# Last half of the output projection: first weight sums by VectorE, six more raw buffers, and a look-ahead of fourteen pieces

## The chip, the cores and the metric

The kernel runs on one core of a Trainium2 chip. Its time is the device time of one execution in microseconds (us), and a run is described by the median of several executions. PE is the matrix engine (TensorE; PEld are its weight loads), DVE is VectorE, ACT is ScalarE, POOL is GpSimd. SP is the engine that issues most of the loads.

## What is computed

One block of a diffusion transformer for 512 latent tokens, 256 context tokens and a width of 2048, all in fp32. What matters here is its end:

```python
y_a = (attn * silu(z_a)) @ w_pa
y_b = (fourier_mix(u_b) * silu(z_b)) @ w_pb
y = (sigmoid(g_a) * y_a + sigmoid(g_b) * y_b) @ w_o
out = rmsnorm(x + gate * y, final_g)
```

The input to `w_o` is called the merged matrix below: 512 tokens by 2048. The output projection is the product of the merged matrix with `w_o` (2048 by 2048). The gates `g_a`, `g_b` come from a product of the same kind, of the normed input with 4096 columns of `w_in`.

## The kernel before

**Every product three times.** An fp32 operand is split into a high part (ScalarE rounds it, line 131) and a low part (VectorE subtracts, line 132). A product is the sum of three matmuls, high by high, high by low and low by high (lines 251 to 253). So each piece of weights, 128 x 1024 or 512 KB, is loaded into a *raw* buffer, split into a pair of tiles (`whi`, `wlo`) and multiplied from there. For a piece of the output projection that is 12 matmuls of 512 columns.

**Seven products for eight.** The gates (four groups, 0 to 3) and the output projection (groups 4 and 5, each half of the columns of `w_o`) are multiplied by a scheme of the Strassen kind: 1024 x 512 blocks of weights are combined, the tokens' matrix is combined into *forms* (A11, Z5, A12, S2, S3, S4, A22), and seven products called P1, Q5, P2, Q6, P7, Q3, Q4 take the place of eight. Each product has four pieces. `class Group` (line 790) runs them; its order in group 5 is `ONE_GROUP`, that of group 4 `OUT_GROUP`. The products of the last group:

- P1 with A11, Q5 with Z5, Q6 with S2 and Q4 with A22 use the weights of a *chain*: four buffers R0 to R3, one for each piece. P1 loads one block into R (line 165, by SP). Q5 needs R plus a second block, Q6 that plus a third, Q4 that plus a fourth.
- P2 (A12) and Q3 (S4) use one block as it is.
- P7 (S3) uses the sum of two blocks: two raw buffers are loaded and VectorE adds them (line 198), then the sum is split.

**Two ways of adding to the chain.** In the general case the next block is added by an accumulating DMA, issued on POOL as soon as R has been split (line 207). For the stages listed in `by_dve`, the block is loaded by SP into a raw buffer like any other, and VectorE adds it to R (line 198) before the split. In the kernel before, the gates do that for stage 1, which is Q5 (`BY_DVE_GATES`), and the output projection for none (`BY_DVE_OUT`).

**The list of pieces.** All pieces, and the blocks of `x` that are added at the end, stand in one list, `todo`, in the order in which they are used. `load_more` moves pieces from its head to `ahead`, up to eight, as long as there are raw buffers for them. `start_load` picks the raw buffers from `raw_pools` by counting which are still held by pieces in `ahead`; a piece whose weights are in R holds none. `get(key)` hands out the next piece: it splits the first few pieces of `ahead` (as many as there are pairs of split tiles, four in the output projection) and starts new loads. A tile's memory is handed on when its last use is over, and each engine's order of issue is made when the kernel is built, from dependencies and the order of the program.

**Raw buffers.** Four in `wp` and two in `rp` exist during the whole second half; two more (`evp`) during the gates, and three more tiles of `hm` (`extra`) during the first three of the four chunks of branch A, which lies between the gates and the output projection. In groups 4 and 5 there are six.

**Tiles for everything else.** `take` and `give` hand out tiles of 4 KB per partition from the list `free`: the oldest free one first. The last group takes tiles from it for its results and for rows of the gate and of the final norm. `free_form` (line 1252) gives back the four tiles of a form when its product in the last group is over.

**The end.** After P2, P7 and Q3, `out_done` multiplies a result by the gate (line 1200), adds `x` (line 1202) and lets `finish_chunk` square it (line 1174) and scale it (line 1180). `prepare` (lines 1185 and 1186) does its part for the results of Q3 and Q4 ahead of time. Lines 821 hold the sums that turn the seven products into results. `last` (lines 1238 to 1249) finishes the last 512 columns for 256 tokens, 128 at a time, and stores them.

```python
part = lambda i: w[CHAIN[i][0], CHAIN[i][1], pc]
stream(key, [part(what)] if what in by_dve else [], 1024, 2, stage=what, pc=pc,
       nxt=part(what + 1) if what < 3 and what + 1 not in by_dve else None)
```

Of the kernel before, what the change touches and what calls it, by code (L numbers as in the profile page):

```python
# [50 lines left out]
ONE_GROUP = ("P1", "Q5", "P2", "Q6", "P7", "Q3", "Q4")  # L51
OUT_GROUP = ("P1", "P2", "Q5", "Q6", "P7", "Q3", "Q4")

BY_DVE_GATES, BY_DVE_OUT = (1,), ()

CHUNKS = (0, 2, 1, 3)
BRANCH_A, BRANCH_B = (0, 1, 2, 3, 4, 5), (6, 7)
# [26 lines left out]
def block_kernel(ctx, tc, xT, ctxT, x, c_row, w_ss, w_gate, vecs, qkg, rope, dft_c, dft_s,  # L84
# [9 lines left out]
    hm = sb("hm", KK)  # L94
# [15 lines left out]
    def uid(s):  # L110
        cnt[0] += 1
        return f"{s}{cnt[0]}"
# [22 lines left out]
    todo, ahead = [], []  # L135
    chain, left = [], [0] * 4
    raw_pools, hl_pools = [(wp, RAW, "raw", RAW)], [wp] * HL
# [11 lines left out]
    def stream(key, src, *a, **k):  # L149
        todo.append(Piece(key, src if isinstance(src, list) else [src], *a, **k))  # L150

    def start_load():

        e = todo[0]
        used = [p for a in ahead for p, _ in a.raws]
        free = [p for p in raw_pools for _ in range(p[1] - used.count(p))]
        if len(e.parts) > len(free) or e.stage == 0 and (not chain or left[e.pc]):
            return False
        todo.pop(0)
        for p, src in zip(free, e.parts):  # L160
            raw = p[0].tile([P, 1024], F32, tag=p[2], bufs=p[3], name=uid("wr"))[:, : e.cols]
            nc.sync.dma_start(raw, src)
            e.raws.append((p, raw))
        if e.stage == 0:
            nc.sync.dma_start(chain[e.pc], e.first)
            left[e.pc] = 1
        ahead.append(e)
        return True

    def load_more():  # L170
        while todo and len(ahead) < 8 and start_load():
            pass

    class Halves:
# [38 lines left out]
    def get(key):  # L213
        load_more()
        turn = [e for e in ahead if not e.aside]
        assert turn[0].key == key, (turn[0].key, key)
        for e in turn[: len(hl_pools)]:
            split_piece(e)
        load_more()
        e = turn[0]  # L220
        ahead.remove(e)
        free.extend(p[0::2] for p, _ in e.raws if p in retired)
        return e.raws[0][1] if e.kind == "raw" else e.out
# [10 lines left out]
    free, retired, home = [], [], {}  # L234
# [4 lines left out]
    def take(shape, dt=F32, pool=None):  # L239
        p = next((p for p in free if p[0] is pool), free[0])  # L240
        free.remove(p)
        t = slot_tile(p, shape, dt)
        home[id(t)] = p, t
        return t

    def give(*ts):
        free.extend(home.pop(id(t))[0] for t in ts)

    def mm3(o, ah, al, bh, bl, start, stop, cont=False):

        nc.tensor.matmul(o, ah, bh, start=start, stop=False, skip_group_check=cont)  # L251
        nc.tensor.matmul(o, ah, bl, start=False, stop=False, skip_group_check=cont)  # L252
        nc.tensor.matmul(o, al, bh, start=False, stop=stop, skip_group_check=cont)  # L253
# [54 lines left out]
    def stream_product(name, g, w, by_dve):  # L308

        what = next(p[2] for p in PRODUCTS if p[0] == name)  # L310
        for pc in range(4):
            key = (name, g, pc)
            if isinstance(what, tuple):
                stream(key, [w[a, b, pc] for a, b in what], 1024, 2)
            else:
# [3 lines that stand above are left out]
                todo[-1].first = part(0)  # L319
# [25 lines left out]
            half, c = DONE[name]  # L345
            stream(("x", half, 2 + c), flat(x[half, 2 + c]), 1024, 1, "raw")
    for name in ONE_GROUP:
        stream_product(name, 5, w_o[0], BY_DVE_OUT)
        half, c = {"P2": (0, 0), "P7": (1, 1), "Q3": (1, 0)}.get(name, (0, 0))
        if name == "Q3":  # L350
            stream(("x", 0, 1), flat(x[0, 1]), 1024, 1, "raw")
            todo.insert(len(todo) - 5, todo.pop())
        if name in ("P2", "P7", "Q3"):
            stream(("x", half, c), flat(x[half, c]), 1024, 1, "raw")
# [260 lines left out]
    for t in range(4):  # L615
        s = slice(t * P, (t + 1) * P)
# [56 lines left out]
    for which, half in ((0, 0), (0, 1), (1, 1)):  # L673
# [3 lines left out]
        for pc in range(8):  # L677
# [3 lines left out]
            for k in range(2):  # L681
                kk = 2 * pc + k
                for a, t in zip(accs, toks):
                    s = slice(t * P, (t + 1) * P) if t < 4 else slice((t - 4) * P, (t - 3) * P)
# [7 lines left out]
        for a, t in zip(accs, toks):  # L692
            a = a.rearrange("p (h d) -> p h d", h=4)
            s = slice(t * P, (t + 1) * P)
# [72 lines left out]
    def pair(tag):  # L767
        return ps2.tile([P, 2, 512], F32, tag=tag, bufs=2, name=uid(tag))
# [8 lines left out]
    def job():  # L777
        if jobs:
            jobs.pop(0)()
# [207 lines left out]
    for i in range(NSTEP + 2):  # L987
# [9 lines left out]
        if i % 3 > 0 and i < 3 * KK:  # L997
            q = i // 3 * 2 + i % 3 - 1
# [3 lines left out]
        if i % 3 < 2 and i < 3 * KK:  # L1002
            q = i // 3 * 2 + i % 3
# [65 lines left out]
    def load_gate(which, half, j):  # L1069
        t = take((2, 512), pool=gp)  # L1070
        nc.gpsimd.dma_start(t, g_d[which, half, j].rearrange("p (t c) -> p t c", t=2))
        return t
# [4 lines left out]
    def turn_merged(j, i, tag):  # L1077

        tp = pair(tag)
        for b in range(2):  # L1080
            for t in range(4):
                c = slice((2 * i + b) * P, (2 * i + b + 1) * P)
                nc.tensor.transpose(tp[:, b, t * P : (t + 1) * P], merged[j, t // 2][:, t % 2, c], ident)
        if i == 0:
            raws[j] = [take((4, 256)) for _ in range(2)]
        else:
            give(merged[j, 0], merged[j, 1])
        for h in range(2):
            nc.scalar.copy(raws[j][h][:, 2 * i : 2 * i + 2, :], tp[:, :, 256 * h : 256 * h + 256])
# [24 lines left out]
    def form_job(name, h):  # L1114
        return lambda: form(name, h)

    extra = [(hm, 1, f"s{i}", 1) for i in range(3)]
    for p in extra:
        free.remove(p[0::2])
    raw_pools += extra  # L1120
    for n, j in enumerate(CHUNKS):
        if n == 3:
            retired += extra
            for p in extra:
                raw_pools.remove(p)
                if not any(q == p for e in ahead for q, _ in e.raws):
                    free.append(p[0::2])
        gb = [load_gate(1, h, j) for h in range(2)]
        ga = [load_gate(0, h, j) for h in range(2)]
        accs = [pair("yx"[n % 2]) for _ in range(2)]  # L1130
        for pc in BRANCH_A:
            if n == 0:
                S[pc] = get(("src", pc))
            wh, wl = get(("pab", j, pc))
            sh, sl = S[pc]
            for t in range(4):
                s = slice(t * P, (t + 1) * P)
                for k in range(2):
                    mm3(accs[t // 2][:, t % 2, :], sh[:, k, s], sl[:, k, s], wh[:, k, :], wl[:, k, :],
                        pc == 0 and k == 0, pc == BRANCH_A[-1] and k == 1)  # L1140
            if pc:
                job()
        for h in range(2):
            nc.vector.tensor_tensor(ga[h], accs[h], ga[h], op=ALU.mult)
            nc.vector.tensor_tensor(gb[h], ga[h], gb[h], op=ALU.add)
            merged[j, h] = gb[h]
        give(*ga)
        turned = [lambda j=j, i=i, n=n: turn_merged(j, i, "yx"[n % 2]) for i in range(2)]
        if n == 3:

            waiting = jobs[:]
            jobs[:] = [lambda: load_rows(1), lambda: None] + turned + [form_job("A12", 1)] + waiting
            jobs.extend(form_job(f, 1) for f in ("Z5", "S2", "S4", "A22"))
        else:
            jobs[:] = turned + jobs
            jobs.extend(form_job(f, j % 2) for f in (("A11", "S3"), ("A12", "Z5", "S2", "S4", "A22"))[j // 2])
# [5 lines left out]
    def load_rows(g):  # L1162
        for l, src in ((gates, gs.rearrange("(o k) p -> o (k p)", o=1)), (fgs, final_g)):
            l[g] = take((2, 512))
            nc.scalar.dma_start(l[g], src[:, 1024 * g : 1024 * g + 1024].broadcast_to([P, 1024]))
# [16 lines left out]
    def prepare(t, half, j):  # L1182

        o[half, j] = t
        nc.vector.tensor_tensor(t, t, row(gates, j), op=ALU.mult)  # L1185
        nc.vector.tensor_tensor(t, get_x(half, j), t, op=ALU.subtract)  # L1186
# [65 lines left out]
    def free_form(name):  # L1252
        for h in range(2):
            give(*held.pop((name, h)))
# [9 lines left out]
    for name in ONE_GROUP:  # L1264
        if name == "Q3":

            nc.scalar.activation(mhalf[:, 8:9], ssq[:, 0, 2:3], ACT.Sqrt)
            prepare(last_group.X, 0, 1)
        elif name == "Q4":
            prepare(last_group.Y, 1, 0)  # L1270
        last_group.run(name)
        free_form(next(f for n, f, _, _ in PRODUCTS if n == name))
        if name == "P1":
            load_rows(0)
    while jobs:
        job()

# [80 lines left out]
```

## Time and profile before

| | us |
|---|---|
| median of 3 runs | 1388.69 |
| lowest, highest | 1388.03, 1389.51 |
| the profiled execution | 1388.98 |
| its span | 1387.2 |
| PE busy | 1351.4 |
| DVE busy | 910.7 |
| ACT busy | 630.1 |

The span is what the profiler recorded from the first to the last instruction of that one execution; the 1.8 us beside it lie before and after. In rows of the timeline the columns are the start, the duration, engine, line, operation, the tile written and the tiles read (buffer numbers left out), and in brackets the idle time of the engine just before and what ended it. Rows of waits give total, count and longest. In the rows of a DMA queue the columns are packets, MB, and the time that the packets took as a share of 16 engines; in rows of DMA issues they are count, KB of each, and median us from issue to landing. The clock is the granted share of TensorE's full clock. A busy time of PE is not PE at its peak, since matmuls are pipelined.

### The profile page before, as it was taken

The numbers are of one execution on the slowest core, as the hardware profiler recorded it, in microseconds if no ns is written. First come the engines' busy times: TensorE is split into PE (matmuls) and PEld (weight loads), VectorE is DVE, ScalarE is ACT, GpSimd is POOL, SyncE is SP. The second block draws the span as 40 slices with busy tenths as digits, with TensorE's granted clock in tenths as the row PEclk, the third lists the DMA queues.
The fourth block names the chain that finished last, engine by engine and source line by source line (L and its number), as shares of the span: only waits on it lengthen the run. The fifth ranks groups of instructions, "written<-read, shape, count | busy, mean of one in ns | idle before, by whom it ended". The sixth has DMA issues, their size and how long they took to land. (4 is left out here: it accounts for less than half of the span.)

```text
span 1387.2 us, 17607 instructions
## 1 busy us (share of the span) xinstructions
PE 1351.4 (97%) x6810; PEld 1107.1 (80%) x6810; DVE 910.7 (66%) x1191; ACT 630.1 (45%) x861; POOL 116.8 (8%) x173
## 2 busy tenths in 40 slices
PE   7999999999999999999999999999999999999986
PEld 4667789888888888888887788888888788878865
DVE  5765486767865668656743776665956546487577
ACT  5322253534545454554544555444544224364434
POOL 0110000011100001000001101000010100020100
PEclk9999999999999999999999999999999999999998
DMA  9887453645443335433447998989898844588973
GB/s 384 330 343 263 168 186 108 185 122 186 153 145 113 116 113 161 140 98 121 124 143 271 326 291 239 258 226 258 263 269 296 310 152 136 136 184 274 238 220 131
DMA packets 76115, 283.67 MB, mean 204 GB/s; under 512 B 8704, under 2 KB 9344, under 8 KB 71680
## 3 DMA queue, kind: packets, MB, share of 16 engines
q1 hardware_dynamic: 52848, 185.28, 39.9%
q0 software_dynamic: 18000, 79.71, 21.2%
q10 hardware_dynamic: 5184, 17.57, 3.3%
q8 instruction: 53, 0.87, 0.3%
q14 instruction: 30, 0.25, 0.1%
HBM read 257.34 MB, written 25.17 MB: 204 GB/s over the span
## 5 line engine op out<-in xcount | busy, mean ns | idle before, releaser
L131 ACT ACTIVATE whi<-wr 128x1024 fp32r<-128x1024 f32 x178 | 185.0, 1043 | 292.7 <-PE pb L252 84.0
L132 DVE TENSOR_TENSOR wlo<-wr,whi 128x1024 fp32r<-128x1024 f32 x178 | 213.4, 1202 | 140.7 <-ACT whi L131 140.5
L251 PE MATMUL pb<-s,whi 128*128 128x512 f32 x512 | 206.7, 405 | 0.6 <-ACT s L415 0.6
L252 PE MATMUL pb<-s,whi 128*128 128x512 f32 x512 | 200.6, 392 | 0.1
L253 PE MATMUL pb<-s,wlo 128*128 128x512 f32 x512 | 200.5, 392 | 0.0
L252 PE MATMUL y<-wlo,s 128*128 128x512 f32 x320 | 127.2, 397 | 7.3 <-DVE wlo L132 7.2
L251 PE MATMUL x<-whi,s 128*128 128x512 f32 x324 | 127.3, 393 | 2.2 <-ACT whi L131 1.1
L252 PE MATMUL x<-wlo,s 128*128 128x512 f32 x324 | 127.2, 393 | 1.9 <-DVE wlo L132 1.9
L251 PE MATMUL y<-whi,s 128*128 128x512 f32 x320 | 126.8, 396 | 0.8 <-ACT whi L131 0.6
L253 PE MATMUL x<-whi,s 128*128 128x512 f32 x324 | 126.9, 392 | 0.0
L253 PE MATMUL y<-whi,s 128*128 128x512 f32 x320 | 126.4, 395 | 0.0
L251 PEld LDWEIGHTS pb<-s,whi 128*128 128x128 f32 x512 | 96.1, 188 | 21.7 <-issue 4.1
L253 PEld LDWEIGHTS pb<-s,wlo 128*128 128x128 f32 x512 | 96.1, 188 | 21.1 <-issue 0.4
L252 PEld LDWEIGHTS pb<-s,whi 128*128 128x128 f32 x512 | 96.4, 188 | 17.1 <-DVE s L416 1.0
L131 ACT ACTIVATE whi<-R 128x1024 fp32r<-128x1024 f32 x66 | 69.6, 1058 | 66.6 <-PE x L253 38.4
L132 DVE TENSOR_TENSOR wlo<-R,whi 128x1024 fp32r<-128x1024 f32 x66 | 80.0, 1219 | 20.5 <-ACT whi L131 20.4
L955 ACT ACTIVATE p<-pd,mx 128x768 f32<-128x768 f32 x48 | 43.2, 899 | 84.9 <-DVE mx L953 84.9
L252 PEld LDWEIGHTS y<-wlo,s 128*128 128x128 f32 x320 | 61.2, 191 | 22.9 <-DVE wlo L132 10.2
L251 PEld LDWEIGHTS x<-whi,s 128*128 128x128 f32 x324 | 61.3, 189 | 16.2 <-ACT whi L131 1.5
L252 PEld LDWEIGHTS x<-wlo,s 128*128 128x128 f32 x324 | 61.2, 189 | 15.2 <-DVE wlo L132 2.6
L251 PEld LDWEIGHTS y<-whi,s 128*128 128x128 f32 x320 | 61.1, 191 | 14.5 <-ACT whi L131 1.0
L253 PEld LDWEIGHTS x<-whi,s 128*128 128x128 f32 x324 | 61.3, 189 | 12.8
(270 smaller groups left out, 2663.7 us busy)
## 6 DMA issues: line engine op xcount, KB each, us to landing
wr<-in_w_g SPq DMA_DIRECT2D x80, 512.0 KB, 8.2
wa<-in_w_ss POOLq DMA_DIRECT2D x28, 1024.0 KB, 8.3
wr<-in_w_m SPq DMA_DIRECT2D x44, 512.0 KB, 3.8
wr<-in_w_gate SPq DMA_DIRECT2D x32, 512.0 KB, 3.6
wr<-in_w_pab SPq DMA_DIRECT2D x32, 512.0 KB, 4.3
R<-in_w_g POOLq DMA_DIRECT2D x32, 512.0 KB, 10.1
wr<-in_w_o SPq DMA_DIRECT2D x32, 512.0 KB, 5.2
wr<-in_w_start SPq DMA_DIRECT2D x26, 512.0 KB, 6.4
```

Source lines behind the costliest of these rows:

```text
L131: nc.scalar.activation(hi, src, ACT.Copy)
L132: nc.vector.tensor_tensor(lo, src, hi.bitcast(F32), op=ALU.subtract)
L251: nc.tensor.matmul(o, ah, bh, start=start, stop=False, skip_group_check=cont)
L252: nc.tensor.matmul(o, ah, bl, start=False, stop=False, skip_group_check=cont)
L253: nc.tensor.matmul(o, al, bh, start=False, stop=stop, skip_group_check=cont)
L955: nc.scalar.activation(p, sc[:, :NKEY], ACT.Exp, bias=mx[:, 0:1], accum_out=mx[:, 1:2])
```

## The change

Three things are changed.

1. The last group (5) gets `BY_DVE_LAST = (1,)`: the block that Q5 adds to the chain is loaded by SP into raw buffers, four of 512 KB, and added by VectorE. The four accumulating DMAs on POOL that did this, issued as P1's pieces were split, are gone. Those for Q6 and Q4 stay, and so do all of group 4.
2. `extra` is written as two helpers, `more_raws` and `fewer_raws`; for branch A they do what was done before. In the last group, `more_raws(3)` is called after P2 and again after Q6: each time the three oldest tiles in `free` become raw buffers. After P2 these are tiles of form Z5, which Q5 used; after Q6 tiles of A12, which P2 used.
3. `load_more` lets up to fourteen pieces be in `ahead` instead of eight. This holds for the whole kernel.

```diff
-BY_DVE_GATES, BY_DVE_OUT = (1,), ()
+BY_DVE_GATES, BY_DVE_OUT, BY_DVE_LAST = (1,), (), (1,)
...
     def load_more():
-        while todo and len(ahead) < 8 and start_load():
+        while todo and len(ahead) < 14 and start_load():
             pass
...
     for name in ONE_GROUP:
-        stream_product(name, 5, w_o[0], BY_DVE_OUT)
+        stream_product(name, 5, w_o[0], BY_DVE_LAST)
...
-    extra = [(hm, 1, f"s{i}", 1) for i in range(3)]
-    for p in extra:
-        free.remove(p[0::2])
-    raw_pools += extra
+    def more_raws(n, pool=None):
+        new = [p for p in free if pool in (None, p[0])][:n]
+        free[:] = [p for p in free if p not in new]
+        new = [(p, 1, tag, 1) for p, tag in new]
+        raw_pools.extend(new)
+        return new
+
+    def fewer_raws(old):
+        retired.extend(old)
+        for p in old:
+            raw_pools.remove(p)
+            if not any(q == p for e in ahead for q, _ in e.raws):
+                free.append(p[0::2])
+
+    extra = more_raws(3, hm)
     for n, j in enumerate(CHUNKS):
         if n == 3:
-            retired += extra
-            for p in extra:
-                raw_pools.remove(p)
-                if not any(q == p for e in ahead for q, _ in e.raws):
-                    free.append(p[0::2])
+            fewer_raws(extra)
...
         if name == "P1":
             load_rows(0)
+        elif name in ("P2", "Q6"):
+            more_raws(3)
```

## The prediction

> **What bounds the kernel now.** I read the totals first, then the span in windows.
>
> ```profile
> span 1387.2 us, 17607 instructions
> PE 1351.4 (97%) x6810; PEld 1107.1 (80%) x6810; DVE 910.7 (66%) x1191; ACT 630.1 (45%) x861; POOL 116.8 (8%) x173
> ```
>
> TensorE (PE) bounds the program: nothing but its idle time, its lost clock and what lies behind its last matmul can be won. The windows say where that is. Columns: stretch, length, busy time of PE, PEld, DVE, ACT, POOL, granted clock, DMA share, GB/s.
>
> ```profile
> 1050.00:1075.00 25.00, 25.00 (x112) 20.71 (x111) 18.65 (x18) 14.03 (x16) 0.00 (x0) 1.00 0.89 305
> ...
> 1325.00:1350.00 25.00, 20.47 (x79) 16.11 (x78) 16.71 (x15) 7.47 (x10) 2.16 (x3) 0.87 0.90 242
> 1350.00:1375.00 25.00, 25.00 (x109) 20.07 (x107) 22.85 (x30) 12.36 (x22) 0.00 (x0) 0.99 0.17 58
> 1375.00:1400.00 25.00, 0.36 (x2) 0.00 (x0) 5.27 (x15) 3.58 (x11) 0.00 (x0) 0.77 0.37 136
> ```
>
> The gate products (first row, one for all of them) keep PE full. In the last group, from about 1290, one window has both a hole and a low clock, and PE ends at 1375.36. The waits of PE from 1320 on, and its timeline, show the hole:
>
> ```profile
> PE y L252 <- DVE wlo L132: 3.8, 2, 3.6
> PE x L252 <- DVE wlo L132: 0.9, 1, 0.9
> ```
> ```profile
> 1336.17 0.39 PE L251 MATMUL y<-whi,s 128*128 128x512 f32 x1
> ...
> 1340.93 0.39 PE L251 MATMUL y<-whi,s 128*128 128x512 f32 x1
> 1344.95 0.79 PE L252 MATMUL y<-wlo,s 128*128 128x512 f32 x1 [3.63 <-DVE wlo L132]
> ...
> 1350.80 0.39 PE L251 MATMUL y<-whi,s 128*128 128x512 f32 x1
> ```
> ```profile
> 1344.40:1347.80 3.40, 2.85 (x7) 0.50 0.72 245
> ```
>
> From 1336.17 to 1340.93 lie 21 matmuls: 0.2267 us each. From 1340.93 to 1350.80 lie 15: at that pace 3.40 us, in fact 9.87. The stall costs **6.47 us**: 3.63 idle, the rest mostly a clock of 0.50 after it. It stands in the last piece of P7, whose weights are a sum of two loads. The chain of waits names the load, with SP's and VectorE's timelines:
>
> ```profile
> 1334.66 7.79 DMA wr<-in_w_o
> ...
> 1342.54 1.22 DVE wr L198
> ```
> ```profile
> 1284.10 0.33 SPq L162 DMA_DIRECT2D wr<-in_w_o  x1
> 1295.11 0.33 SPq L162 DMA_DIRECT2D wr<-in_w_o  x1
> ```
> ```profile
> 1295.00 1.22 DVE L132 TENSOR_TENSOR wlo<-R,whi 128x1024 fp32r<-128x1024 f32 x1
> ...
> 1304.80 1.22 DVE L132 TENSOR_TENSOR wlo<-R,whi 128x1024 fp32r<-128x1024 f32 x1 [3.91 <-ACT whi L131]
> ...
> 1318.37 1.23 DVE L198 TENSOR_TENSOR wr<-wr,wr 128x1024 f32<-128x1024 f32 x1 [6.51 <-DMA wr<-in_w_o]
> ...
> 1333.41 1.22 DVE L132 TENSOR_TENSOR wlo<-wr,whi 128x1024 fp32r<-128x1024 f32 x1
> ...
> 1378.01 0.75 DVE L1238 TENSOR_TENSOR s<-y,s 128x256 f32<-128x256 f32 x2
> ```
>
> The late load was issued at 1334.66, just as a split that began at 1333.41 (1.22 us long) gave its raw buffer back. So **a lack of raw buffers** (six here) made it late, and 7.79 us of transfer followed. Two DMA rows for 1284 to 1312 show why a transfer takes that long:
>
> ```profile
> q0 software_dynamic: 1043, 3.82, 73.5%
> q1 hardware_dynamic: 398, 1.43, 14.9%
> ...
> R<-in_w_o POOLq DMA_DIRECT2D x8, 512.0 KB, 10.9
> wr<-in_w_o SPq DMA_DIRECT2D x5, 512.0 KB, 9.1
> ```
>
> In these 28 us the accumulating queue (q0) held the engines for 20.6 us to move 3.82 MB, SP's queue (q1) 4.2 us for 1.43 MB: for 512 KB (0.524 MB) 2.8 against 1.5 us.
>
> **The change part by part.**
>
> *The four sums of Q5.* Removed: four accumulates on POOL, part of the eight above; four times 2.8 is 11.3 us of engine time gone from the fullest stretch. Added: four SP loads, 6.1 us of engine time. They don't need R, so they can take the buffers that the kernel before filled with P2's first weights and x ahead of P1's four R loads, and they land before the congestion. P2's four then take the buffers freed at 1284.10, at 1295.11 and by Q5's adds (about 1297 and 1300). With the median of 9.1 us the last lands near 1309; P2 is multiplied from about 1312, its last piece from about 1320. Nothing is late.
>
> *Four adds on VectorE.* Each is an L198 of 1.23 us (the row of 1318.37), so 4.9 us in all. Behind each add stand the split of its piece, and through it PE. Q5's first matmul starts here:
>
> ```profile
> 1301.18 0.39 PE L251 MATMUL x<-whi,s 128*128 128x512 f32 x1
> ```
>
> A piece is 12 matmuls, 2.72 us, so the low halves are due near 1301.4 and, for the fourth, 1309.6. The splits end at 1296.2 (1295.00 + 1.22) and 1306.0. The first has 5.2 us of slack and needs 1.2; the fourth has 3.6 and a 3.91 us idle gap ahead of it, 7.5 together against 4.9. Its cost on the path is 0; without the gap it is 1.3. Each split is also what lets POOL start the next accumulate, for Q6; up to 2 us later there is hidden behind P2's 48 matmuls (10.9 us).
>
> *Six more raw buffers.* They join after P2 and after Q6 in the text, but lie in tiles of forms that are dead earlier: the first three in Z5's, dead when Q5 ends (1301.18 + 10.9, about 1312). By the order in which buffers are dealt they get the two parts of P7's last piece and an x. So the load of 1334.66 can go out near 1312, 22 us earlier, and is due on VectorE near 1339. The next three, A12's, free near 1323, take an x and Q3's first two pieces. No row shows a load into such a tile. From below: it goes at 1312 and the stall is gone (6.47 us). From above: it stands in SP's order behind others and still goes at 1334.66 (0). I take the first: at 9.1 us per transfer it would have to be issued 18 us later than possible before it hurts.
>
> The 0.9 us stall is a Q6 split behind an add that waited for P7's third pair; the same relief touches it, but VectorE's order may keep it: I count half, 0.45.
>
> *Fourteen pieces instead of eight.* This works on the whole kernel. But SP waits for buffers, not for the list:
>
> ```profile
> SPq L162 <- DVE wlo L132: 595.7, 153, 22.3
> ```
> ```profile
> 1056.93 0.33 SPq L165 DMA_DIRECT2D R<-in_w_o  x1
> ...
> 1148.95 0.33 SPq L162 DMA_DIRECT2D wr<-in_w_pab  x1
> ```
>
> The R load stands behind every in_w_pab load in the list of pieces, and yet it went out 92 us ahead of the last of them, with all of them for the last chunk still to come: the order of issue is not the list's, and a load already runs ahead of the limit when its buffer is free. I take 0. Bounds: one stall like the one above either way, minus 6.5 to plus 6.5 us.
>
> *What is late next.* VectorE. It works through the last products without a gap after 1342.54, and its final product for the last tokens starts at 1378.01, 2.65 us behind PE's end. Its idle waits before that (3.91 and 6.51 among them) go too, so it should be less behind: I take half, 1.3 us, bounds 0 and 2.65.
>
> **Sum:** 6.47 + 0.45 + 1.3 = 8.2 us. The profiled execution took 1388.98 us (span 1387.2 plus 1.8 around it), 0.29 above the median of 1388.69. 1388.69 - 8.2 = **1380.5 us**.
>
> The Trainium skill speaks against one term. *DMA: Bandwidth & Descriptors*, section *Issuing engines are not separate DMA queues*, says that transfers of all issuing engines share 16 DMA engines, so that moving one between queues saves only the time to initiate it. The row differs: 2.8 against 1.5 us of engine time, because the moved one no longer accumulates. By the rule the relief would be nothing and the sum would rest on the buffers alone; the first rival below is what it would then look like.
>
> **The rivals.**
>
> *The transfer is late anyway.* If P7's last pair waits for DMA engines rather than buffers, issuing early only queues it. For: DMA share 0.90 in the window of the stall, 9.1 us per load. Against: the load was issued in the very moment a buffer came free, and was needed at once. Then the stall stays, with the small terms lost too: 1388.7, between 1386 and 1391.
>
> *VectorE becomes the end.* Four more adds, and splits in order behind adds that wait for DMA (6.51 us at 1318.37). If it keeps its 2.65 us delay and PE keeps one hole of 2 to 3 us, too short for the clock to fall, the gain is 8.2 - 1.3 - 0.45 - 2.5, about 4: 1384.7.
>
> *The deeper look-ahead reorders the gate products: slower.* The fourteen shift SP's order where DMA is 0.89 busy and PE has no slack; a chain load R or an accumulate goes out behind prefetched weights, and PE waits at a boundary between groups. Price 6.5 us each, decided by whether the wait is long enough to bring the clock to 0.50. One leaves 1387; from two on it is slower, 1380.5 + 13 = 1393.5. Against: the early R load above.
>
> **How the numbers follow.** Forecast (stall gone) 0.60, with its own range 1377 to 1383; VectorE at the end 0.17; late anyway 0.10; slower 0.13. No change means within 0.2% (2.8 us, about what a measurement of this kernel tells from nothing). Faster: 0.60 + 0.17 = 0.77; same 0.10; slower 0.13. The range starts at 1376.5, where VectorE's delay and an early stall go as well, and reaches 1389, across the case of the late transfer.
>
> **What would show it.** In the changed trace: no accumulates between about 1285 and 1293, four L198 near 1290 to 1305 with no PE wait behind them; P7's last pair issued before 1325; no window with a clock of 0.50 in the last group; PE's end near 1368. Wrong would be: a wait of PE on VectorE's split of over 3 us in P7 or Q3; VectorE's final product over 3 us behind PE; or new PE waits before 1080, which would put the blame on the fourteen.

## The result, and the profile after

The changed kernel takes **1395.59 us** (median of 7 runs, 1392.43 to 1400.29) against 1388.69 of the kernel before on the same chip (7 runs, 1386.47 to 1390.76): ratio 1.0053, 95% interval 1.0034 to 1.0072. It is slower by about 7 us. The forecast was 1380.5, the range went from 1376.5 to 1389, and slower had a chance of 0.13.

The profiled execution took 1392.43 us, the shortest of the seven: it shows 3.7 us of the 6.9 between the medians (1392.43 against 1388.69), and the rest is in no profile. The totals of the changed kernel's page:

```profile
span 1390.7 us, 17602 instructions
...
PE 1352.0 (97%) x6810; PEld 1108.8 (80%) x6810; DVE 914.8 (66%) x1195; ACT 630.8 (45%) x861; POOL 113.5 (8%) x169
```

TensorE does the same work, VectorE four instructions more, GpSimd four fewer. The windows of the changed kernel, columns as in the prediction:

```profile
750.00:775.00 25.00, 18.60 (x77) 14.29 (x76) 12.07 (x12) 10.91 (x15) 0.00 (x0) 0.95 1.02 406
775.00:800.00 25.00, 25.00 (x103) 20.47 (x102) 18.58 (x18) 15.14 (x18) 4.03 (x5) 0.91 0.98 285
1050.00:1075.00 25.00, 25.00 (x112) 20.71 (x111) 17.43 (x17) 13.07 (x15) 1.10 (x2) 1.00 0.76 259
1075.00:1100.00 25.00, 21.21 (x82) 16.71 (x81) 10.57 (x9) 8.25 (x8) 2.10 (x4) 0.86 0.86 327
1325.00:1350.00 25.00, 21.45 (x86) 17.29 (x87) 18.75 (x17) 7.88 (x11) 3.45 (x4) 0.93 1.00 298
1350.00:1375.00 25.00, 25.00 (x111) 20.51 (x110) 22.92 (x24) 10.89 (x18) 0.00 (x0) 1.00 0.05 18
1375.00:1400.00 25.00, 4.83 (x21) 3.60 (x20) 8.90 (x24) 6.85 (x17) 0.00 (x0) 0.82 0.46 168
```

Three of these stretches of the kernel before were not shown ahead of the prediction:

```profile
750.00:775.00 25.00, 22.79 (x91) 17.53 (x90) 14.86 (x15) 13.74 (x19) 0.90 (x1) 0.93 1.03 412
775.00:800.00 25.00, 22.58 (x99) 18.02 (x98) 17.58 (x18) 13.82 (x17) 4.34 (x6) 1.00 0.91 272
...
1075.00:1100.00 25.00, 23.49 (x96) 18.70 (x95) 10.67 (x9) 8.14 (x8) 3.17 (x6) 0.93 0.86 314
```

Count the matmuls: 91 and 99 became 77 and 103 between 750 and 800, where the gate products begin, and 96 became 82 from 1075 on, where branch A begins. In the window from 1325 on 79 became 86, but the last group's waits are not smaller: 2.54 and 2.38 us, 4.92 together, against 0.89 and 3.63, 4.52 together, before. What is smaller is the loss of clock (0.93 against 0.87). The matmuls of the changed kernel that waited over half a microsecond, from its timeline (in brackets the wait and what ended it):

```profile
761.54 0.50 PE L251 MATMUL x<-whi,s 128*128 128x512 f32 x1 [0.65 <-ACT whi L131]
762.99 0.50 PE L252 MATMUL x<-wlo,s 128*128 128x512 f32 x1 [0.95 <-DVE wlo L132]
771.76 0.50 PE L251 MATMUL x<-whi,s 128*128 128x512 f32 x1 [3.26 <-ACT whi L131]
773.81 0.79 PE L252 MATMUL x<-wlo,s 128*128 128x512 f32 x1 [1.55 <-DVE wlo L132]
1085.67 0.50 PE L251 MATMUL y<-whi,s 128*128 128x512 f32 x1 [1.86 <-ACT whi L131]
1088.10 0.79 PE L252 MATMUL y<-wlo,s 128*128 128x512 f32 x1 [1.93 <-DVE wlo L132]
1251.93 0.50 PE L251 MATMUL x<-whi,s 128*128 128x512 f32 x1 [1.10 <-ACT s L827]
1326.17 0.50 PE L252 MATMUL y<-wlo,s 128*128 128x512 f32 x1 [2.54 <-DVE wlo L132]
1342.49 0.79 PE L252 MATMUL x<-wlo,s 128*128 128x512 f32 x1 [2.38 <-DVE wlo L132]
```

And of the kernel before (the last one, of 3.63 us at 1344.95, stands in the prediction):

```profile
761.82 0.49 PE L251 MATMUL x<-whi,s 128*128 128x512 f32 x1 [1.13 <-ACT whi L131]
763.27 0.76 PE L252 MATMUL x<-wlo,s 128*128 128x512 f32 x1 [0.96 <-DVE wlo L132]
798.26 0.50 PE L252 MATMUL y<-wlo,s 128*128 128x512 f32 x1 [2.25 <-DVE wlo L132]
1081.77 0.49 PE L251 MATMUL y<-whi,s 128*128 128x512 f32 x1 [0.55 <-ACT whi L131]
1083.22 0.50 PE L252 MATMUL y<-wlo,s 128*128 128x512 f32 x1 [0.95 <-DVE wlo L132]
1246.19 0.50 PE L251 MATMUL x<-whi,s 128*128 128x512 f32 x1 [1.10 <-ACT s L827]
1330.15 0.50 PE L252 MATMUL x<-wlo,s 128*128 128x512 f32 x1 [0.89 <-DVE wlo L132]
```

The rows of 1246.19 and 1251.93 are the same matmul of group 4. With it the span falls into two parts that every kernel here can be read by. **Part A**, from the wait for a low half at the start of the gates (763.27; 762.99) to that matmul: 482.92 us before, 488.94 after, 6.0 lost. **Part B**, from there to PE's end (1375.36; 1379.83): 129.17 and 127.90, 1.3 won. What follows PE's end went from 11.8 to 10.9. So what this profile shows of the loss lies in part A, in code that only the fourteen pieces touch.

### The profile page after: what moved, and what is told of

It is laid out like the page before. It is cut to its first block, busy times and chain, and to the rows that moved or that the text cites. A ratio compares the mean times of both kernels' runs of the same rounds, so it can differ in the third digit from the quotient of the medians.

```text
span 1390.7 us, 17602 instructions
## 1 busy us (share of the span) xinstructions
PE 1352.0 (97%) x6810; PEld 1108.8 (80%) x6810; DVE 914.8 (66%) x1195; ACT 630.8 (45%) x861; POOL 113.5 (8%) x169
```

## The experiments

Ratios are against the kernel before on the same chip, 5 rounds each. One profile per kernel gives A and B, in us. Kernels that are alike in a part differ there too: by up to 4.9 us in A (480.1 to 485.0 with eight pieces) and by some 3 us in B. So only large differences are read, and the times decide.

| kernel | median us | ratio (95%) | A | B |
|---|---|---|---|---|
| before | | 1 | 482.9 | 129.2 |
| changed | 1395.59 | 1.0053 (1.0034-1.0072) | 488.9 | 127.9 |
| changed, eight | 1385.03 | 0.9986 (0.9976-0.9996) | 482.7 | 127.2 |
| before, fourteen | 1392.33 | 1.0038 (1.0024-1.0052) | 489.1 | 129.6 |
| sums alone | 1387.89 | 1.0018 (1.0007-1.0028) | 481.7 | 130.5 |
| raws alone | 1384.15 | 0.9985 (0.9976-0.9993) | 483.1 | 126.6 |
| raws, order of adds | 1385.96 | 0.9983 (0.9973-0.9992) | 484.5 | 127.3 |
| eight, order of adds | 1387.76 | 1.0000 (0.9988-1.0011) | 480.1 | 128.7 |
| eight, fourteen late | 1389.16 | 1.0011 (1.0000-1.0022) | 481.1 | 129.6 |
| before, fourteen at the gates | 1391.47 | 1.0029 (1.0017-1.0041) | 484.7 | 128.2 |
| eight, new first | 1383.34 | 0.9950 (0.9932-0.9969) | 481.5 | 123.7 |
| raws, new first | **1380.62** | **0.9939** (0.9918-0.9961) | 481.8 | 122.6 |
| eight, new first, order | 1381.25 | 0.9942 (0.9924-0.9960) | 485.0 | 121.6 |
| raws, new first, order | 1381.52 | 0.9942 (0.9923-0.9961) | 484.1 | 121.6 |
| before, fourteen after the gates | 1389.77 | 1.0003 (0.9989-1.0017) | 486.0 | 126.4 |
| changed, new first | 1389.32 | 1.0008 (0.9992-1.0023) | 488.8 | 124.9 |
| before, fourteen, one load moved | 1394.57 | 1.0044 (1.0029-1.0058) | 488.0 | 127.1 |
| before, fourteen, old deal | 1389.62 | 1.0012 (0.9999-1.0026) | 484.3 | 127.5 |

### The three changes apart

The changed kernel with the look-ahead put back:

```diff
-        while todo and len(ahead) < 14 and start_load():
+        while todo and len(ahead) < 8 and start_load():
```

> The changed kernel with the look-ahead back at eight pieces; VectorE's sums for Q5 and the six raw buffers stay. Theory A (the fourteen cost some 5.7 us before the last group, the rest of the change wins 2 to 5 us): 1384 to 1387 us, the waits of PE near 772 and 1086 us back at about 1 us each, no weights of P2 loaded ahead of Q5's at the start of the gates. Rival B (the look-ahead costs nothing, the new sums and loads of the last group are what makes it slower): about 1395, and the stretch up to 1246 as in the changed kernel.

Measured: 0.9986. The waits at the gates and at branch A are those of before, and part A is as long as before.

The kernel before with that one line the other way round:

> The kernel before with nothing but the look-ahead raised to fourteen. Theory A: 1394 to 1397 us, with PE waiting some 3 us for a split by ScalarE near 772 us and some 4 us near 1086, and the stall of P7 in the last group still there. Rival B: 1388.7, within 0.2%.

Measured: 1.0038, with all of the loss in part A. The waits named for the gates and branch A came (2.94 us at 770.02, 1.62 and 1.93 near 1086), and P7's stall is still there (3.56 us).

The sums of Q5 by VectorE, without new buffers and with eight:

```diff
-        stream_product(name, 5, w_o[0], BY_DVE_OUT)
+        stream_product(name, 5, w_o[0], BY_DVE_LAST)
```

> Look-ahead eight, no more raw buffers: only the four sums of Q5 move to VectorE. Theory A (a lack of raw buffers makes P7's last pair late): the four loads take buffers and P7's last pair is as late as before or later, so 1388 to 1393 us with a stall of 3 us or more in P7. Rival C (the accumulating transfers make all loads slow, so that removing four of them is what helps): 1381 to 1385.

Measured: 1.0018, slightly slower, though the stall in P7 came out smaller than was expected: 1.63 us. A new wait of 2.27 us stands at 1316.48, for a split of P2.

The six buffers, eight pieces, accumulates as before (the helper `more_raws` is that of the change):

```diff
         if name == "P1":
             load_rows(0)
+        elif name in ("P2", "Q6"):
+            more_raws(3)
```

> Look-ahead eight, accumulating transfers as before: only the six raw buffers of the last group are added. Theory A: P7's last pair is issued before 1325 us and the 3.6 us stall with its slow clock is gone; VectorE's add for P7 stands ahead of one split of P2 as before, so at most 1 us per hold: 1381 to 1385 us. Rival D (the stall only moves to another split behind an add that waits for its loads): 1386 to 1390, with a PE wait of 2 to 4 us on VectorE between 1320 and 1346.

Measured: 0.9985. The time is the one that theory A gave, but TensorE waits as the rival said, 1.53 and 2.84 us behind adds of P7. So the fourteen cost 5.3 us in the kernel before (0.0038 of 1386.4), the buffers bring 2 us, and the sums bring nothing: alone they cost 2.5 us, beside the buffers 0 (0.9986 against 0.9985).

### What was left of the last group's gain

The buffers should have brought 6.5 us. VectorE's adds (L198) and SP's loads of the changed kernel show where it stuck:

```profile
1290.98 1.23 DVE L198 TENSOR_TENSOR R<-R,wr 128x1024 f32<-128x1024 f32 x1
...
1302.34 2.35 DVE L198 TENSOR_TENSOR R<-R,wr 128x1024 f32<-128x1024 f32 x2
1323.75 1.23 DVE L198 TENSOR_TENSOR wr<-wr,wr 128x1024 f32<-128x1024 f32 x1 [8.88 <-DMA wr<-in_w_o]
...
1338.94 1.23 DVE L198 TENSOR_TENSOR wr<-wr,wr 128x1024 f32<-128x1024 f32 x1 [5.43 <-DMA wr<-in_w_o]
```
```profile
1312.60 0.39 SPq L162 DMA_DIRECT2D wr<-in_w_o  x1
...
1315.32 0.41 SPq L162 DMA_DIRECT2D wr<-in_w_o  x1
...
1327.28 0.33 SPq L162 DMA_DIRECT2D wr<-in_w_o  x1
1327.70 0.38 SPq L162 DMA_DIRECT2D wr<-in_x  x1
1331.27 0.33 SPq L162 DMA_DIRECT2D wr<-in_w_o  x1
```

By the order of SP's instructions, 1312.60 and 1315.32 are P7's *last* piece (P7_3), the one that was late before. 1327.28 and 1331.27 are the two halves of P7_2, which is needed earlier and now comes last of the four, with two loads of x ahead of its second half. The add of 1338.94 is P7_2's and waits for that second half. The add of 1323.75 is P7_0's; its second half, too, had to wait for an old buffer and went out at 1312.18. Both long adds have another piece's low split behind them on VectorE: TensorE's waits of 2.54 (behind the add of 1323.75) and 2.38 (behind that of 1338.94). The stall did not go; it became two. With eight pieces the same two adds wait, but only the first delays TensorE:

```profile
1316.80 1.23 DVE L198 TENSOR_TENSOR wr<-wr,wr 128x1024 f32<-128x1024 f32 x1 [8.92 <-DMA wr<-in_w_o]
...
1338.75 1.23 DVE L198 TENSOR_TENSOR wr<-wr,wr 128x1024 f32<-128x1024 f32 x1 [4.64 <-DMA wr<-in_w_o]
```

Is it the place of the adds, or are the loads late? Each add of P7 was put behind the low split of the piece before it (`lows` is the list of the low splits):

```diff
-        nc.vector.tensor_tensor(lo, src, hi.bitcast(F32), op=ALU.subtract)
+        lows.append(nc.vector.tensor_tensor(lo, src, hi.bitcast(F32), op=ALU.subtract).ins)
...
-            nc.vector.tensor_tensor(src, src, r, op=ALU.add)
+            with tc.issue_after(lows[-1]) if e.key[:2] == ("P7", 5) else ExitStack(): nc.vector.tensor_tensor(src, src, r, op=ALU.add)
```

> Six more raw buffers, eight pieces, weight sums by DMA as before, and each add of P7 in the last group put behind the low split of the piece before it on VectorE (with raws alone the adds of 1318.53 and 1331.42 waited 7.87 and 4.86 us for their loads, and TensorE waited 1.53 and 2.84 us for low splits behind them). Theory C (an in-order engine behind an add that waits for its load is the cost): both TensorE waits fall to under 0.7 us, the time is 3 to 4.5 us below raws alone, about 1380.5, ratio 0.9955 to 0.9970. Rival (the loads themselves are late, and P7's own splits then wait as long): TensorE waits of 2 us or more stand in P7, and the time is within 1 us of raws alone, 1384.

> The changed kernel with eight pieces and each add of P7 in the last group put behind the low split of the piece before it (there: one TensorE wait of 2.59 us at 1319, behind the add that waited 8.92 us). Theory C: the wait goes, no TensorE wait over 1 us in the last group before its end, 1382 to 1383 us, ratio 0.997. Rival (the loads are late): the wait moves to P7's own low splits, 1385. A rival of the end: VectorE has the adds later in P7, so that an evacuation or a split of Q3 is late, and the time is 1385 or above.

Measured: 0.9983 and 1.0000. The first wait goes, but a wait for P7's own split stands where the second was: 2.70 us instead of 2.84 without the sums, with them 4.09 us, where no wait over half a microsecond had stood. With the changed kernel's sums and eight:

```profile
1338.56 1.23 DVE L198 TENSOR_TENSOR wr<-wr,wr 128x1024 f32<-128x1024 f32 x1 [7.00 <-DMA wr<-in_w_o]
```
```profile
1340.99 0.79 PE L251 MATMUL y<-whi,s 128*128 128x512 f32 x1 [4.09 <-ACT whi L131]
```

The rival holds: the loads are late, whatever the adds do. But why, if buffers are free? Because of the deal. `raw_pools.extend(new)` puts the new buffers last, so P7_0 to P7_2 take old ones, which come free late, and P7_3, x and Q3 take the new ones, which come free early; the loads stand in SP's queue in the order in which their buffers come free. The next kernels change that one line:

```diff
-        raw_pools.extend(new)
+        raw_pools[:] = raw_pools + new if pool else new + raw_pools
```

> The changed kernel with eight pieces, and the six new raw buffers put ahead of the old ones in the list from which a piece takes them, so that the pieces P7_2 and P7_3, both second halves included, are queued on SP ahead of the loads of x and of Q3 (with the new buffers last, the second half of P7_2 stood behind P7_3's pair, two loads of x and two of Q3, and its add at 1338.75 had waited 4.64 us). Theory C' (the order in which SP hands out the loads, while the DMA is full from 1300 to 1340, makes the second wait; VectorE's order makes the first): the wait of 2.59 at 1319 for the low split behind P7_0's add stays, the add of P7_2 waits under 1 us, the time is that of the changed kernel with eight or up to 1 us less, ratio 0.998 to 0.999. Rival (x or Q3 come too late in turn): a new TensorE wait over 1 us after 1345, ratio 1.000 or more.

> Six more raw buffers alone, eight pieces, the new ones ahead of the old ones. Theory C': of the TensorE waits of raws alone (1.53 at 1321, 2.84 at 1335) the second goes, the first stays, 2 us below raws alone, ratio 0.9965 to 0.9975. Rival (transfers as such are the limit): both stay, ratio 0.9985.

> The changed kernel with eight pieces, the new buffers first, and each add of P7 behind the low split of the piece before it. Theory C': with the order alone the one wait left was for P7_2's second half (4.09 us of TensorE at 1341, its add had waited 7.00 us); with the loads of P7 queued ahead of x and Q3 that wait goes too, no TensorE wait over 1 us stands in the last group, and the time is 3 to 4 us below that with the order alone, ratio 0.997 to 0.998. Rival (the transfers as such are the limit): a TensorE wait of 2 us or more stays in P7, ratio 1.000.

> Six more raw buffers, eight pieces, weight sums by DMA as before, the new buffers first, and each add of P7 behind the low split of the piece before it. Theory C': no TensorE wait over 1 us in the last group, the lowest time of all, 2.5 to 4 us below raws alone, ratio 0.9955 to 0.997. Rival (the transfers as such are the limit): a wait of 2 us or more stays in P7, ratio 0.998 or above.

Measured: 0.9950, 0.9939, 0.9942, 0.9942. All four are 7 to 8.5 us below before (ratio times 1389.13), more than was expected of the line. VectorE's adds (grouped), the idle time ahead of them, and an SP row of the buffers alone, new first:

```profile
L198 DVE TENSOR_TENSOR wr<-wr,wr x4: 1217/1218/1225, 1318.1 to 1324.9; 128x1024 f32<-128x1024 f32 x4
...
  DMA wr<-in_w_o: 7.8, 1
```
```profile
1319.32 0.33 SPq L162 DMA_DIRECT2D wr<-in_w_o  x1
1319.74 0.38 SPq L162 DMA_DIRECT2D wr<-in_x  x1
```

The last load of P7 goes out at 1319.32, ahead of every load of Q3 and of the x blocks that stand behind P7 in the list, the four adds are over at 1326.1 (1324.9 + 1.2), and TensorE has one wait left in part B, 1.50 us at 1320. B falls by 6.6 us against before. With the order of the adds as well that wait goes too; A came out longer in those two profiles, and the times are the same. The buffers alone, new first, have the lowest ratio, though the four intervals overlap; neither the sums nor the fourteen are in it. Not all of the gain is seen as waits: with the sums and eight, TensorE's one long wait of 2.6 us near 1319 is the same with the new buffers first as with them last, and yet part B is 3.5 us shorter (123.7 against 127.2). Some of that is the clock behind this wait in the one profile of each: 0.56 for 2 us with the new buffers last, 1.00 with them first.

The Trainium skill, *DMA: Bandwidth & Descriptors*, section *Queues, rings and completion order*, says that an engine takes the descriptors of one queue in the order in which they were put in. These runs agree: P7_2's add waits 4.64 us with its second half behind x and Q3, and no longer with it ahead.

### Where the fourteen cost

The limit was made a variable that changes at one place: `limit[0] = 14` where the last group begins (first run below), or 14 up to Q5 of the first gate group and 8 from there, or 8 up to there and 14 from there. The second of these, against the kernel before:

```diff
-    todo, ahead = [], []
+    todo, ahead, limit = [], [], [14]
...
-        while todo and len(ahead) < 8 and start_load():
+        while todo and len(ahead) < limit[0] and start_load():
...
             if (g, name) == (0, "Q5"):
-                hl_pools += range(MORE_HL)
+                hl_pools += range(MORE_HL); limit[0] = 8
```

> The changed kernel with eight pieces until the last group begins and fourteen from there. Theory A (the fourteen cost at the start of the gates and of branch A, where they deal raw buffers out anew, and do nothing for the last group): the TensorE waits at 761 to 798 and 1082 to 1084 are those of before, the time is that of the changed kernel with eight, 1385 (1384 to 1386), ratio 0.999. Rival B' (it is in the last group that the fourteen cost): 1388 or above, ratio 1.002 or more. Rival B'' (fourteen bring the last group forward): below 1383.5.

The changed kernel with eight until the last group begins: 1.0011, against 0.9986 with eight throughout. Fourteen cost about 3.5 us there (0.0025 of 1387.6), where the expectation was nothing. SP's order shows one load of Q3 more ahead of P7_2's second half; its add waits for it, 7.18 us instead of 4.64, and at 1346 TensorE then waits 1.09 and 0.76 us for P7's splits:

```profile
1343.74 1.23 DVE L198 TENSOR_TENSOR wr<-wr,wr 128x1024 f32<-128x1024 f32 x1 [7.18 <-DMA wr<-in_w_o]
```

> The kernel before with fourteen pieces up to the start of Q5 in the first gate group and eight from there. Theory A in two places: only the loss at the gates is left (TensorE waits near 770 and 772 as with fourteen throughout), the waits at 1082 and 1083 are those of before, the first group of the output projection starts 2.6 us later than before rather than 5.7 us, and the time is about 1389 (1388.3 to 1390), ratio 1.002 (with fourteen throughout 1.0038). Rival (the loss at branch A follows from the one at the gates, not from the look-ahead there): the wait at 1084 is there all the same, ratio 1.004. Second rival (what is lost at the gates is caught up later): ratio 1.000.

> The kernel before with eight pieces up to the start of Q5 in the first gate group and fourteen from there (the other half of the run with fourteen in the gates' start alone, which gave 1.0029). Theory A in places: the waits near 770 and 772 are gone, those at 1084 and 1087 (1.62 and 1.93 with fourteen throughout) are there, and what is left of fourteen's 1.0038 is 1.001 to 1.002. Rival (all of fourteen's cost is made at the gates): ratio 1.000 or less. Second rival (what fourteen cost does not add up by places): 1.003 or more.

The kernel before with fourteen up to Q5 of the first gate group, and with fourteen from there on: 1.0029 and 1.0003. By these times most of the loss is made at the gates' start. The profiles are less clear: that of the first, its fastest execution, has waits of 1.07 and 1.56 us near 770 and 772 where 2.94 and 1.55 were expected, and a part A only 1.8 us longer than before, within what A varies. At branch A the first of them has a wait of 2.25 us at 1083.82, though the order of its loads there is that of before, so a wait of that size can come by chance. The second lengthens part A by 3.1 us, with a wait of 1.95 us at 1086, but its part B came out shorter, and its time shows no loss that can be told from none. What the fourteen cost at branch A stays open, between 0 and 3 us.

At the gates' start ScalarE's split of a piece of P2 stands in its order ahead of a split that P1 needs, and waits for its load; before and after:

```profile
765.68 0.63 ACT L131 ACTIVATE s<-wr 128x512 fp32r<-128x512 f32 x1 [2.49 <-DMA wr<-in_w_g]
```
```profile
770.13 0.63 ACT L131 ACTIVATE s<-wr 128x512 fp32r<-128x512 f32 x1 [7.22 <-DMA wr<-in_w_g]
```

The load is P2_1's. Its place in SP's queue is one later than before, since P2_2's load has moved ahead of the four loads into R. First I took that place for the cause and moved the one load of P2_2 behind P2_1's:

```diff
-            nc.sync.dma_start(raw, src)
+            with tc.issue_after(was[0]) if e.key == ("P2", 0, 2) else ExitStack(): was[0] = nc.sync.dma_start(raw, src).ins
```

> The kernel before with fourteen pieces throughout, and one single load moved in SP's queue: that of P2_2 of the first gate group, which with fourteen stands ahead of the four loads into the forms, is put behind P2_1's, so that P2_1's load is one place earlier again. Theory A' (the gates' start loses because P2_1's load, one place later in a stretch where the DMA is full, lands 4.4 us later, and ScalarE's split of it stands ahead of P1_3's): the TensorE wait of 2.94 at 770 falls under 1 us, the time is 2 to 3 us below fourteen throughout, ratio 1.0015 to 1.0025. Rival (it is the loads of Q5, dealt behind the forms' loads, or the fuller DMA itself): the wait of about 3 us stays, ratio 1.0035 or more.

Measured: 1.0044, no better; TensorE still waits 1.97 us at 770.65 (2.94 without the move). That theory fell. What stands between the loads into R and P2_1's is the same with this load moved as without. It is the deal again. By the kernel's own choice of buffers, with eight Q5_2 and Q5_3 take two of the first four raw buffers, P2_0 and P2_1 the pool `rp`; with fourteen the choice is made earlier in the text, when those four still count as held, so Q5_2 and Q5_3 take `rp`, P2_0 and P2_1 `evp`. Q5_2's load then no longer goes out ahead of R's, but behind. So the last kernel keeps the limit of fourteen and makes Q5_2 and Q5_3, and with them whatever stands behind them in the list, wait for one of the first four:

```diff
-        if len(e.parts) > len(free) or e.stage == 0 and (not chain or left[e.pc]):
+        if len(e.parts) > len(free) or e.stage == 0 and (not chain or left[e.pc]) or e.key in (("Q5", 0, 2), ("Q5", 0, 3)) and free[0][0] is not wp:
```

> The kernel before with fourteen pieces throughout, but the two pieces Q5_2 and Q5_3 of the first gate group wait, as with eight, for a buffer of the first four raw ones, so that the pieces from Q5_2 to P2_3 get the buffers that they have with eight, and Q5_2's load again stands ahead of the four loads into the forms, in a stretch where the DMA has room. Theory A'' (not the depth but the deal of the buffers makes the loss at the gates): the waits of 2.94 at 770 and 1.55 at 772 go, and the time is that of fourteen from Q5 on (ratio 1.0003), at most 1.0015. Rival (the depth as such, a fuller DMA): the waits stay, ratio 1.003 or more.

Measured: 1.0012, and the split is back where it was, with TensorE's waits at 770 and 772 gone:

```profile
765.62 0.63 ACT L131 ACTIVATE s<-wr 128x512 fp32r<-128x512 f32 x1 [2.29 <-DMA wr<-in_w_g]
```

So at the gates it is which buffer each piece is dealt, and not the limit as such: with the same limit of fourteen the ratio is 1.0012 (0.9999 to 1.0026) in place of 1.0038. (At those two pieces the edit holds back the list as well as the deal, and the two were not told apart.) Two windows of the kernel before suggest why the place ahead of R's loads is worth so much:

```profile
735.00:745.00 10.00, 10.00 (x57) 8.67 (x56) 2.12 (x3) 2.46 (x4) 0.01 (x1) 1.00 0.54 186
...
750.00:760.00 10.00, 10.00 (x45) 7.99 (x44) 2.70 (x3) 2.54 (x5) 0.00 (x0) 1.00 1.02 408
```

Q5_2's load went out at 735.77, ahead of R's at 743.99, to engines that were half idle (DMA share 0.54); behind R's it queues at 1.02.

> The changed kernel as it is, fourteen pieces too, with the new raw buffers ahead of the old ones. Theory C' (the waits of the last group come from P7's loads standing behind P7_3's, x's and Q3's): the waits of 2.38 at 1342 and of what follows it in P7 go, the last group is 5 us shorter, while the losses at 772 and 1086 stay: 5 us above the changed kernel with eight and the new buffers first, ratio 0.998 to 1.000. Rival (with fourteen the deal of the buffers does no good, since more loads of Q3 are queued anyway): ratio 1.003 or above.

The changed kernel as it is, new buffers first: 1.0008, against 0.9950 with eight: the fourteen cost 8 us in this pairing, where 5 were expected, and part A has its 488.8 back. The wait at 1342 went, as expected, and part B fell by 3 us (124.9 against 127.9). The right deal in the last group and the wrong one at the gates cancel.

**The loss summed up.** Eight with sums and buffers 0.9986; fourteen at the gates +0.0029; fourteen in the last group +0.0025; together 1.0040. The rest to 1.0053 is within the interval; branch A's waits would fit. The sum is rough: the last term was measured with a load of Q3 ahead of P7_2's second half, and in the changed kernel none stands there.

## Why the prediction was wrong, point by point

**The step that failed is the one on the fourteen pieces:** "the order of issue is not the list's, and a load already runs ahead of the limit when its buffer is free. I take 0." SP does wait for buffers, as the row of 595.7 us showed; but the limit decides when, in the text, a piece is *given* its buffer, and with that which load waits for what. The early R load showed only that loads overtake one another. Measured: 5.3 us in the kernel before, which the bound of 6.5 holds; beside the rest of the change 9.3 us (1.0053 against 0.9986) and 8 us (1.0008 against 0.9950, each of these pairs from two chips), which it does not. The rival "the deeper look-ahead reorders the gate products" named the place almost rightly (the start of the gates and of branch A rather than the boundaries between gate groups). It asked for two waits that bring the clock to 0.50 and charged 6.5 us for each. Two such places came, each with two waits of 1.5 to 3.3 us and a clock of 0.50 behind them (from 773.81 and from 1088.10), but part A lost 6.0 us by both together. That the rival's 1393.5 lies near the measured time is luck: it starts from a gain of 8.2 us that did not come. Nor did the gate products keep PE full, as one window was taken to show for all of them: the kernel before already waits 2.25 us at 798.26.

The miss of 15.1 us is made of two steps: some 9 us for the fourteen, forecast at 0, and some 6 us of the forecast gain of 8.2 that the rest of the change did not bring (0.9986 is 1.9 us).

**The six buffers were the right mechanism at the wrong size.** The prediction read from the deal that P7's last piece would get the new buffers and took that as the whole remedy: 6.47 us. The pair was issued at 1312.60 and 1315.32, and P7_2's second half at 1331.27. Part B starts 5.7 us later in the changed kernel; with that taken off, the pair went out at 1306.9 and 1309.6, somewhat ahead of the forecast's 1312, but P7_2's second half at 1325.5, only 9 us sooner than the late load of 1334.66. The term measured 2.1 us with this deal and 8.5 us (0.9918 to 0.9961: 5.4 to 11.4) with the new buffers first. The upper bound that was written down, "it stands in SP's order behind others", was true of a neighbouring piece. The question that the prediction put, "What is late next", was answered with VectorE; the answer was P7_2.

**The four sums of Q5.** Right where the prediction looked: no accumulate is issued between 1280 and 1300, POOL is empty there, and TensorE does not wait behind the adds at 1290.98 to 1302.34.

```profile
1280.00:1290.00 10.00, 10.00 (x45) 8.18 (x44) 8.49 (x8) 4.47 (x7) 0.00 (x0) 1.00 0.75 239
1290.00:1300.00 10.00, 10.00 (x46) 8.15 (x45) 9.97 (x9) 5.38 (x8) 0.00 (x0) 1.00 0.57 179
```

Engine time is freed (DMA share 0.57 from 1290 to 1300, where it was 1.04 before). It was worth nothing: from 1290 to 1315 SP waits 7.6 us in all for buffers that Q5's adds give back, and in no pair of runs did the sums help. Nor was their cost on the path 0. With the sums, and the adds in their own order, two low splits of P2 stand on VectorE behind P7_0's add and not one, and TensorE's wait there is 2.27 to 2.60 us in all six such kernels; without the sums it is at most 1.53. The rule that the prediction cites from the Trainium skill, *DMA: Bandwidth & Descriptors*, section *Issuing engines are not separate DMA queues*, gave the right outcome, no relief, though not for its reason, since engine time was freed.

**The 0.45 for the Q6 split** went the other way: the wait for a split of Q6 behind the add of P7's third piece was 0.89 and is 2.38. The wait of 2.54, behind the add of the first piece, is for a split of P2 and is new. **VectorE's end**, 1.3 us: its final product starts 1.89 us behind PE's end (1381.72 against 1379.83) instead of 2.65, so 0.76 won; the span's tail shrank by 1.0. **The transfer that is late anyway**, given 0.10, was nearer to the outcome in the last group than the forecast, but not for its reason: what made loads late was which buffer they were dealt and so their place in the queue.

**The signs named in advance.** "New PE waits before 1080, which would put the blame on the fourteen" is what the trace shows at 771.76 and 773.81, and the blame was right. "No window with a clock of 0.50" did not hold in the last group; no wait there exceeds 3 us, but there are two, and behind the second the clock falls:

```profile
1342.49:1345.49 3.00, 3.00 (x7) 2.42 (x8) 2.59 (x3) 1.85 (x5) 0.86 (x1) 0.50 1.03 273
```

PE's end, forecast near 1368, came at 1379.83; the buffers alone with the right deal end at 1367.2.

## What to carry to other kernels

A look-ahead limit and the end of a list at which new buffers are put look like mere capacity, but where buffers are dealt when the program is built, they decide which load waits for which release. Before more buffers are costed, write down for each piece which buffer it gets and when that comes free: the buffers free first must go to the pieces needed first. And a stall in an in-order queue has a successor: look for the next late load among the neighbours of the one that is repaired, not only at the end.

## What was not expected of the hardware

The waits that bring a slow TensorE are not those above a fixed length. A matmul took 0.79 us instead of 0.50 after single waits of 3.63 (before) and 4.09 us (1340.99, eight with the order of adds), but also, in the changed kernel, at 773.81, after 3.26 and 1.55 us two microseconds apart, and at 1088.10, after 1.86 and 1.93; after a single wait of 2.54 (1326.17) it did not, and after 2.38 at 1342.49 it did. The granted clock agrees: 0.50 for 2 us from 773.81 and from 1088.10, 1.00 from 1326.17. The slow stretch can also begin behind the wait: in the kernel before, matmuls took 0.50 us right after the waits of 0.55 and 0.95 at 1081.77 and 1083.22, but the clock was 0.50 from 1084.29 to 1087.20. The prediction had made the price hang on one long wait, and took a hole of 2 to 3 us as too short for the clock to fall. The Trainium skill, *TensorE: Matmul & The Clock Gate*, section *HAM oscillation — how this bites in real kernels*, names gaps of over about 3.4 us; the rows here show the clock falling after shorter ones as well, so the measurement decides.

A load that is handed over a little later in a stretch where the DMA is full can land much later: P2_1's split began 4.45 us later (770.13 against 765.68) in the changed kernel for one more 512 KB load behind R's, which at 406 GB/s take 1.3 us. What makes up the rest was not settled.
